# Gate weight sums by accumulating DMAs, and the fourth product added to the finished output

## The chip, the cores and the metric

The kernel runs on one core of a Trainium2 chip. The metric is the device time in microseconds (us) of one execution, the median of three runs. The core has TensorE (PE, with its weight loads PEld), VectorE (DVE), ScalarE (ACT), GpSimd (POOL) and SyncE (SP), and 16 DMA engines, which queues of SP, ACT and POOL feed. Each engine takes its instructions in order.

## The reference

One layer on x of 1024 tokens by 1024 channels in fp32. Two branches read the same normalised input, and per-channel gates merge them:

```python
xn = rmsnorm(x, norm1_g[layer])
u = xn @ w_in[layer].astype(f32)
...
o_sb = merge_heads(stick_breaking_attention(...))     # 8 heads of 64, in blocks of 128 queries
...
o_hg = rmsnorm(o_hg, ...)                             # HGRN2, 4 heads of 128
o_hg = merge_heads(o_hg) * jax.nn.silu(g_hg)
g_a = jax.nn.sigmoid(gate_sb + bg[:D_MODEL])
g_b = jax.nn.sigmoid(gate_hg + bg[D_MODEL:])
merged = g_a * (o_sb @ w_o_sb[layer]) + g_b * (o_hg @ w_o_hg[layer])
h = x + merged @ w_out[layer]
hn = rmsnorm(h, norm2_g[layer])
a = jnp.square(jax.nn.relu(hn @ w_ff1[layer]))
h = h + a @ w_ff2[layer]
return rmsnorm(h, final_g)
```

gate_sb, gate_hg (1024 columns each) and g_hg (512) are slices of u. They are matrix products of xn with columns of w_in, and these products are what the change is about.

## The kernel before, in words

**Products.** A matrix product in fp32 is made of three: both operands are split into a high part, which ACT copies (`hi_copy`), and a low part, which DVE subtracts (`lo_sub`), and PE adds up high x high, low x high and high x low in a PSUM bank of 128 x 512.

**Stages.** The program runs through: normalisation and transposes; attention, 8 heads of 8 query blocks, 64 items; HGRN2, head by head; the gates with the merge; the output product; the two MLP products; the last normalisation. Products that do not depend on the attention (the projections, the jobs `raw_job`, `q_job`, `f_job`) are laid in between the items by `st.advance`.

**The gates.** The columns of a gate product are taken in pairs of 128 columns: pair cb from 0 to 7 takes 128 columns of gate_sb and the same 128 of gate_hg; pairs 8 and 9 take four blocks of g_hg. The 2 x 2 block product (two halves of the 1024 rows of w_in, two column blocks, two halves of the tokens) is made by seven products in place of eight, which needs sums of the weights and of the inputs. The first half of the work (class `RawUnit`, `raw_job(cb)`), products 1, 2 and 4, runs early, beside attention and HGRN2; its results go to DRAM (`pd`, `gd`). The second half (class `GatePair`) runs in the gate stage with products 6, 5, 7 and 3: `x6`, `y5`, `x7`, `y3`. x6 and x7 add up in the bank gX, y5 and y3 in the bank gY, each of 12 matmuls. `RawUnit` subtracts weights on DVE into product 4's operand, in steps 4, 6 and 8 of the job (`split_t`); `GatePair.split` makes three subtractions of 512 columns on DVE for each pair. The inputs' sums (`sum_forms`) are made once. After x7 the sums with p1 and p14, which come back from DRAM as the tile pr, are made by DVE; after y3 the sum with u2 (gu).

**The order.** The pairs run 8, 9, 0, 4, 1, 5, 2, 6, 3, 7. For a pair of 0 to 7 an output product of the HGRN2 branch (`hg_product`, bank pyh, 12 matmuls) stands between x7 and y3. For pair 9 nothing stands there. Work of the next pair (the splits into tg, whig, wlog) is put behind `y_sum`, the first sum after x7. A scheduler sorts each engine's instructions by the dependencies and by those that `after` adds.

**POOL's queue.** In the attention POOL issues the copies that double a head's Q (L698: QH and QL, two halves of each head), clears small tiles, and issues the sums of the output weights (`out_weight_sums`, L1320: 32 DMAs of 256 KB into tw in DRAM, of which the last 16 add to what is there), one for every second item. A DMA that adds to a tile waits on POOL until the one before into this tile has landed.

Of the kernel before, what the change touches and what calls it, by code (L numbers as in the profile page):

```python
# [2 lines left out]

# [16 lines left out]
P = 128  # L20
# [19 lines left out]
def kernel(  # L40
# [462 lines left out]
    class Stream:  # L503
# [36 lines left out]
        def step(self):  # L540

            if self.gen is None:
                if self.pos >= len(self.jobs):
                    return False
                self.steps = 0
                self._start()
            self.steps += 1
            if self.owed_t and self.steps in (4, 6, 8):
                self.owed_t.split_t(hg_level[0] or turn_lo[0], self.steps // 2 - 1)
                if self.steps == 8:  # L550
                    self.owed_t = None
# [760 lines left out]
    def out_weight_sums():  # L1312
# [3 lines left out]
        for op, ways in ((ALU.bypass, plain), (ALU.add, summed)):  # L1316
            for i, src in ways:
                for r in range(4):
                    rs = slice(r * P, (r + 1) * P)
                    after(nc.gpsimd.dma_start(tw[i][rs], src[rs], accum_op=op), lastsel[0])  # L1320
                    yield

    def gate_bias(which, cb):
        return prm[:, BG + which * KT + cb : BG + which * KT + cb + 1]
# [8 lines left out]
    class RawUnit(Unit):  # L1333


        late = True
        turned = 0

        def __init__(self, cb):
            dmas = [  # L1340
                [(0, P, W_IN[:, gate_cols(w, cb)].rearrange("(k p) c -> p k c", p=P))]
                for w in range(2)
            ]
            super().__init__(f"wga{cb}", dmas)
            if cb < KT:
                self.roomy = (1,)

        def split(self):
            if self.hl is not None:
                return  # L1350
            self.load()
            ra, rb = self.raw
# [3 lines left out]
            hi_lo(h, l, ra)  # L1356
            self.hl = [(h, l)]

        def split_t(self, behind=None, upto=3):
            ra, rb = self.raw  # L1360
            while self.turned < upto:
                self.turned += 1
                if self.turned == 1:
                    after(sub(rb, ra, rb), behind)
                elif self.turned == 2:
                    after(sub(rb[:, 512:], rb[:, 512:], rb[:, 0:512]), behind)
                else:
                    t = slot(f"{self.name}t", F32R)
                    self.hl.append((t[:, 0:512], t[:, 512:]))
                    after(hi_lo(*self.hl[1], rb[:, 512:]), behind)  # L1370

    raw_units = [RawUnit(cb) for cb in range(NG)]

    def raw_job(cb):
# [13 lines left out]
        def body():  # L1388
            p1, p14, g1 = (half(f"{n}_{cb}") for n in ("p1", "p14", "g1"))
            ps, p4 = bank(f"pga{cb}"), bank(f"pgq{cb}")  # L1390
# [12 lines left out]
            hi_behind[0] = None  # L1403
            yield from steps_of(p4, 1, 0, 1, 4, True)
            add(p14, p1, p4)
            if cb == 3 or cb == KT - 1:
                whole_input(1, int(cb == KT - 1))
            nc.gpsimd.dma_start(pd[cb][:, 1, :], p14)
# [27 lines left out]
    def sum_forms():  # L1436
# [93 lines left out]
    class GatePair:  # L1530
# [3 lines left out]
        def load(self):  # L1534
# [3 lines left out]
            ]  # L1538
            for i, s_, which in ((0, 0, 0), (0, 1, 1), (1, 1, 1)):
                load(  # L1540
                    self.raw[i][:, s_ * 512 : (s_ + 1) * 512].rearrange("p (k c) -> p k c", k=4),
                    W_IN[i * 512 : (i + 1) * 512, gate_cols(which, cb)].rearrange(
                        "(k p) c -> p k c", p=P
                    ),
                )
            if cb >= KT:
# [17 lines left out]
        def split(self, behind=None):  # L1564
            cb = self.cb
            r0, r1 = self.raw
            s0, s1 = slice(0, 512), slice(512, 1024)
            first = behind if self is gates_in[3] else None
# [74 lines left out]
        def x7(self):  # L1643
            self.product(7, self.X, False)
            p1, p14 = self.p[:, 0:512], self.p[:, 512:1024]
            self.y_sum = add(p1, p1, self.Y)
            add(p1, p1, self.X)
            add(p14, p14, self.X)
            self.gate(p1, 1)
            self.gate(p14, 0)  # L1650

        def late_half(self):
# [3 lines left out]
            ps = self.hg_product(1)  # L1656
            p1, p14, y = self.p[:, 0:512], self.p[:, 512:1024], self.y[:, 512:1024]
            mul(y, y, p14)
            mul(p1, p1, ps)
# [749 lines left out]
    for h in range(NHG + 1):  # L2409
# [4 lines left out]
        while going:  # L2414
            going = False
            for g in (lev, tail):
# [112 lines left out]
```

## Time and profile before

| | |
|---|---|
| median of 3 runs | 1419.76 us (1419.64 to 1419.85) |
| the profiled execution's span | 1418.4 us, 18800 instructions |
| PE busy | 1408.7 us, 99% |
| DVE busy | 1086.9 us, 77% |
| ACT busy | 684.9 us, 48% |
| POOL busy | 147.3 us, 10% |
| granted TensorE clock, mean | 0.999 |
| HBM | 168.32 MB read, 66.06 MB written |

The median is 1.36 us above the span of the profiled execution; that much lies around the first and the last instruction. Times in the trace count from the start of the span. In a row of a timeline stand start, us, engine, line, operation, output <- input, and in brackets an idle time ahead of it with what ended it. In the chain of waits the pieces follow one another without gaps.

### The profile page before, as it was taken

To read this page: it belongs to the slowest core of one execution; us is meant where nothing else is said; L and a number is where in the kernel's file an instruction comes from. 1 tells how busy PE (TensorE), PEld (TensorE's weight loads), DVE (VectorE), ACT (ScalarE), POOL (GpSimd) and SP (SyncE) were. 2 spreads that over 40 slices of the span, in tenths; PEclk is the share of its full clock that TensorE was granted. 3 is DMA by queue.
4 is the path that set the end of the run, shared out by engine and by line. 5 is a ranking of instruction groups with operands and counts; after the bars stand their busy time and mean duration, and the time that the engine had idled before them with its cause. 6 is when DMAs were issued, how large, how long until landed. Compare 5 with 4: busy or idle time off the path is not lost.

```text
span 1418.4 us, 18800 instructions
## 1 busy us (share of the span) xinstructions
PE 1408.7 (99%) x6848; PEld 1183.6 (83%) x6848; DVE 1086.9 (77%) x1493; ACT 684.9 (48%) x1183; POOL 147.3 (10%) x341
## 2 busy tenths in 40 slices
PE   9999999999999999999999999999999999999998
PEld 7888888888888888888888888888888888888886
DVE  7679988988567888887788897676666657668765
ACT  6356676664243554433344764445444443534343
POOL 3012223210011031000000300000000000000042
PEclk9999999999999999999999999999999999999999
DMA  7124445535135685364585514444446974776725
GB/s 238 30 67 127 105 100 98 107 77 157 59 74 171 224 225 178 126 215 156 162 298 193 186 54 169 163 163 143 137 145 239 353 265 149 279 273 238 278 94 188
DMA packets 163173, 237.72 MB, mean 168 GB/s; under 512 B 26332, under 2 KB 93448, under 8 KB 163080
## 3 DMA queue, kind: packets, MB, share of 16 engines
q1 hardware_dynamic: 146056, 190.37, 40.0%
q0 software_dynamic: 11584, 34.61, 10.0%
q10 hardware_dynamic: 5440, 11.54, 2.3%
q8 instruction: 54, 0.88, 0.3%
q14 instruction: 39, 0.32, 0.1%
HBM read 168.32 MB, written 66.06 MB: 165 GB/s over the span
## 4 chain that ended last, share of the span: by engine, by line
PE 98%; DVE 1%; ACT 0%; POOL 0%; DMA 0%; issue 0%; POOLq 0%; SPq 0%; DVEq 0%
PE pm L128 21%; PE pX L128 9%; PE pW L128 6%; PE pY L128 6%; PE pjqk L128 6%; PE pga L128 4%; PE gX L128 4%; PE gY L128 4%; PE pjf L128 3%; PE pjq L128 3%; PE pys L128 3%; PE pji L128 3%; PE pyh L128 3%; PE pjv L128 3%; PE po L128 3%; PE z L128 2%
## 5 line engine op out<-in xcount | busy, mean ns | idle before, releaser
L156 ACT CAST whid<-w 128x1024 fp32r<-128x1024 f32 x30 | 31.6, 1053 | 154.5 <-PE pm L128 87.4
L831 DVE TENSOR_TENSOR_SCAN rm<-rm,bits 128x511 f32<-128x511 f32 (+7 forms) x72 | 87.3, 1219 | 16.4 <-ACT rm L809 16.4
L128 PE MATMUL pm<-wlod,sh 128*128 128x512 f32 x240 | 93.5, 390 | 0.0
L128 PE MATMUL pm<-whid,sl 128*128 128x512 f32 x240 | 93.4, 389 | 0.0
L128 PE MATMUL pm<-whid,sh 128*128 128x512 f32 x240 | 93.4, 389 | 0.0
L128 PE MATMUL pm<-tl,sh 128*128 128x512 f32 (+1 forms) x210 | 81.3, 387 | 0.0
L128 PE MATMUL pm<-th,sl 128*128 128x512 f32 (+1 forms) x210 | 81.3, 387 | 0.0
L128 PE MATMUL pm<-th,sh 128*128 128x512 f32 (+1 forms) x210 | 81.3, 387 | 0.0
L161 DVE TENSOR_TENSOR wlod<-w,whid 128x1024 fp32r<-128x1024 f32 x30 | 36.7, 1222 | 55.3 <-ACT whid L156 55.3
L161 DVE TENSOR_TENSOR sl<-sa,sh 128x1024 fp32r<-128x1024 f32 x56 | 68.2, 1218 | 0.0
L156 ACT CAST wTh<-pw 128x512 fp32r<-128x512 f32 (+2 forms) x96 | 43.8, 485 | 41.9 <-PE pw L131 41.0
L2148 POOL TENSOR_SCALAR fss<-fss 128x1 f32<-128x1 f32 x8 | 4.5, 561 | 562.0 <-ACT fsc L2143 561.5
L156 ACT CAST sh<-sa 128x1024 fp32r<-128x1024 f32 x56 | 57.2, 1046 | 7.2 <-DMA sa<-ad 7.2
L161 DVE TENSOR_TENSOR wTl<-pw,wTh 128x512 fp32r<-128x512 f32 (+2 forms) x96 | 49.9, 546 | 4.6 <-ACT wTh L156 4.4
L128 PEld LDWEIGHTS pm<-wlod,sh 128*128 128x128 f32 x240 | 45.1, 188 | 10.0 <-DVE wlod L161 0.4
L128 PEld LDWEIGHTS pm<-whid,sh 128*128 128x128 f32 x240 | 45.0, 188 | 9.5
L128 PEld LDWEIGHTS pm<-whid,sl 128*128 128x128 f32 x240 | 45.0, 188 | 9.1
L169 DVE TENSOR_TENSOR bt<-bt,rm 128x511 f32<-128x511 f32 (+7 forms) x72 | 48.9, 684 | 3.5
L809 ACT ACTIVATE rm<-z 128x511 f32<-128x511 f32 (+4 forms) x96 | 48.0, 500 | 5.5 <-PE z L128 2.8
L128 PE MATMUL pX<-sqh,t1l 128*128 128x512 f32 x128 | 49.9, 390 | 0.0
L128 PE MATMUL pX<-sql,t1h 128*128 128x512 f32 x128 | 49.9, 390 | 0.0
L128 PE MATMUL pX<-sqh,t1h 128*128 128x512 f32 x128 | 49.8, 389 | 0.0
(932 smaller groups left out, 4434.8 us busy)
## 6 DMA issues: line engine op xcount, KB each, us to landing
w<-in_w_ff_dram SPq DMA_DIRECT2D x72, 512.0 KB, 4.8
sa<-ad SPq DMA_DIRECT2D x52, 512.0 KB, 6.4
ad<-a SPq DMA_DIRECT2D x32, 256.0 KB, 4.3
ad<-s SPq DMA_DIRECT2D x16, 512.0 KB, 3.3
tw<-in_w_out_dram POOLq DMA_DIRECT2D x24, 256.0 KB, 4.6
pr<-pd SPq DMA_DIRECT2D x10, 512.0 KB, 6.0
x<-in_x_dram SPq DMA_DIRECT2D x8, 512.0 KB, 7.8
xnl<-xnh POOLq DMA_DIRECT2D x8, 512.0 KB, 6.5
```

The source lines that it names most:

```text
L128: return pe(nc.tensor.matmul(*a, **k))
L156: hi_last[0] = after(in_turn("act", nc.scalar.copy(dst, src)), hi_behind[0])
L161: nc.vector.tensor_tensor(out=dst, in0=src, in1=hi.bitcast(F32), op=ALU.subtract),
L169: return nc.vector.tensor_tensor(out=out, in0=a, in1=b, op=ALU.mult)
L809: nc.scalar.activation(rm[:, s0 + c0 - 1 : s0 + m - 1], z[:, c0:m], AF.Sigmoid, scale=-0.125)
L831: sc = nc.vector.tensor_tensor_scan(out=rr, data0=rr, data1=bits[:, 1024 - nk + a : 1024 - nk + b][:, ::-1], initial=rm[:, b : b + 1] if i ...
L2148: nc.gpsimd.tensor_scalar(out=ssq, in0=ssq, scalar1=1.0 / D, scalar2=EPS, op0=ALU.mult, op1=ALU.add)
```

## The change

It does four things.

1. The sums of weights for the gates are made in DRAM by DMAs of POOL, `gate_weight_sums`: 43 DMAs of 512 KB into tg1 to tg4 (tg1 and tg3 lie in one tensor tg13), one after each item of the attention. First come four for the g_hg columns of tg4 (one writes, three add), then 32 for the blocks of 128 x 1024, then seven for the g_hg columns of tg1, tg3 and tg2. The 32 DMAs for the output weights follow behind, also one by one, the last of them in the loop over the HGRN2 heads.
2. The signs are turned so that all sums of weights are additions: `sum_forms` and the sums after the products get other signs. DVE's subtractions of weights go; `RawUnit` loads 512 and 256 KB in place of 1 MB, `GatePair` 512, 256 and 256 KB, and `split_t` runs once, in step 6.
3. The fourth product goes to DRAM by itself (p4, copied by ACT) instead of added to the first (p14, added by DVE). In `x7` it is added to the finished p1.
4. `raw_job(KT)` and `q_job(0)` change places among the jobs of heads 2 and 4.

**POOL around the first copies of head 1.** tg4 is the tile of the new sums in DRAM, tw that of the output weights' sums, QH1 and QL1 are head 1's copies, two halves each. Rows of small memsets are left out. Before:

```order
L698 DMA QH1_874<-QH1_874 64x512 [waits DVE_49,Activation_49]
L698 DMA QL1_875<-QL1_875 64x512 [waits DVE_49,PE_49]
L1320 DMA tw_131<-in_w_out_dram 128x512
L698 DMA QH1_874<-QH1_874 64x512 [waits Activation_49]
L1320 DMA tw_131<-in_w_out_dram 128x512 [waits DMASW0_49]
L698 DMA QL1_875<-QL1_875 64x512 [waits DMASW1_49,DVE_49]
```

Now:

```order
L1337 DMA tg4_144<-in_w_in_dram 512x2x128
L698 DMA QH1_876<-QH1_876 64x512 [waits DVE_49,Activation_49]
L698 DMA QL1_877<-QL1_877 64x512 [waits DVE_49,PE_49]
L1337 DMA tg4_144<-in_w_in_dram 512x2x128 [waits DMASW4_49]
L1337 DMA tg4_144<-in_w_in_dram 512x2x128 [waits DMASW7_49,DMASW0_49]
L698 DMA QH1_876<-QH1_876 64x512 [waits DMASW1_49,Activation_49]
L1337 DMA tg4_144<-in_w_in_dram 512x2x128 [waits DMASW2_49,DMASW0_49]
L698 DMA QL1_877<-QL1_877 64x512 [waits DMASW3_49,DVE_49]
```

Before, two writes to tw that wait for nothing but a free semaphore stood between the copies; now three DMAs that add to tg4 stand there, each waiting for a DMA ahead of it, and the last copy of QL1 stands behind the third of them.

**DVE after x7 of pair 9.** pr9 holds p1 and p4 (p14), gX9 and gY9 are the banks, gu9 is u2, tgl0 a weight split of the next pair, ahgl1 a part of HGRN2's output. Before:

```order
L1289 TENSOR_TENSOR pr9_5777<-pr9_5777,gY9_5916 128x512 [waits DVE_49,PE_49]
L161 TENSOR_TENSOR ahgl1_5913<-on1_4493,ahgh1_5912 128x1024 [waits Activation_49]
L161 TENSOR_TENSOR tgl0_5937<-wg0r0_5781,tgh0_5936 128x1024 [waits Activation_49]
L1289 TENSOR_TENSOR pr9_5777<-pr9_5777,gX9_5891 128x512 [waits DVE_49,PE_49]
L1289 TENSOR_TENSOR pr9_5777<-pr9_5777,gX9_5891 128x512
L1289 TENSOR_TENSOR gu9_5904<-gu9_5904,gY9_5916 128x512 [waits PE_49]
```

Now:

```order
L162 TENSOR_TENSOR ahgl1_5933<-on1_4536,ahgh1_5932 128x1024 [waits Activation_49]
L162 TENSOR_TENSOR tgl0_5954<-wg0r0_5801,tgh0_5953 128x1024 [waits DMAHW5_49,Activation_49]
L1289 TENSOR_TENSOR pr9_5797<-pr9_5797,gX9_5911 128x512 [waits PE_49]
L1289 TENSOR_TENSOR pr9_5797<-pr9_5797 128x512 [waits DVE_49]
L1292 TENSOR_TENSOR pr9_5797<-gY9_5936,pr9_5797 128x512 [waits DVE_49]
L1292 TENSOR_TENSOR gu9_5924<-gY9_5936,gu9_5924 128x512 [waits PE_49]
```

Before, gY9 was read ahead of the two splits and gX9 twice after them; now gX9 is read once, the second sum is of pr9 alone, and gY9 is read third. y3 adds into gY9 and waits for that.

**DVE after x7 of pair 0.** wg4 holds the weights of pair 4, the next one, wlog4 and tgl4 are its splits. Before:

```order
L1289 TENSOR_TENSOR pr0_5944<-pr0_5944,gY0_6019 128x512 [waits DVE_49,PE_49]
L161 TENSOR_TENSOR ahgl3_6016<-on3_5494,ahgh3_6015 128x1024 [waits Activation_49]
L1289 TENSOR_TENSOR pr0_5944<-pr0_5944,gX0_5994 128x512 [waits DVE_49,PE_49]
L1289 TENSOR_TENSOR pr0_5944<-pr0_5944,gX0_5994 128x512
L1292 TENSOR_TENSOR wg4r0_5948<-wg4r0_5948 128x512 [waits DMAHW7_49,DMAHW6_49]
```

Now:

```order
L162 TENSOR_TENSOR ahgl3_6033<-on3_5520,ahgh3_6032 128x1024 [waits Activation_49]
L1289 TENSOR_TENSOR pr0_5961<-pr0_5961,gX0_6011 128x512 [waits PE_49]
L162 TENSOR_TENSOR wlog4_6067<-wg4r1_5966,whig4_6066 128x1024 [waits DMAHW7_49,DMAHW0_49]
L1289 TENSOR_TENSOR pr0_5961<-pr0_5961 128x512 [waits DVE_49]
L162 TENSOR_TENSOR tgl4_6071<-wg4r0_5965,tgh4_6070 128x1024 [waits DMAHW6_49,Activation_49]
L1292 TENSOR_TENSOR pr0_5961<-gY0_6036,pr0_5961 128x512 [waits DVE_49]
```

Before, gY0 was read ahead of gX0. Now the two splits of pair 4 stand between the three sums, and the read of gY0 is the last.

The diff, cut to its core:

```diff
-            if self.owed_t and self.steps in (4, 6, 8):
-                self.owed_t.split_t(hg_level[0] or turn_lo[0], self.steps // 2 - 1)
-                if self.steps == 8:
-                    self.owed_t = None
+            if self.owed_t and self.steps == 6:
+                self.owed_t.split_t(hg_level[0] or turn_lo[0])
+                self.owed_t = None
...
+    TGW = NG * P
+    tg13 = dram("tg13", [1024, TGW])
+    tg = {1: tg13[0:512], 3: tg13[512:1024]}
+    tg.update({i: dram(f"tg{i}", [512, TGW]) for i in (2, 4)})
+
+    def gate_weight_sums():
+        def gh(i, which):
+            rows = W_IN[i * 512 : (i + 1) * 512, C_GH : C_GH + HGW]
+            return rows.rearrange("k (c w p) -> w k c p", w=2, p=P)[which]
...
+        def add_up(dst, src, op=ALU.add):
+            after(nc.gpsimd.dma_start(dst, src, accum_op=op), lastsel[0])
+
+        for t, terms in (
+            (4, ((0, 0), (0, 1), (1, 0), (1, 1))),
+            (1, ((0, 0), (0, 1))),
+            (3, ((0, 1), (1, 1))),
+            (2, ((0, 0), (0, 1), (1, 1))),
+        ):
+            if t == 1:
+                yield from block_sums(range(4))
+            for j, (i, which) in enumerate(terms):
+                add_up(gh_of(tg[t]), gh(i, which), ALU.add if j else ALU.bypass)
+                yield
+
+    def block_sums(rows):
...
+        for t, op, src in (
+            (1, ALU.bypass, (0, 0)),
+            (3, ALU.bypass, (0, 1)),
+            (1, ALU.add, (0, 1)),
+            (3, ALU.add, (1, 1)),
+            (2, ALU.bypass, 1),
+            (2, ALU.add, (1, 1)),
+            (4, ALU.bypass, 2),
+            (4, ALU.add, (1, 0)),
+        ):
+            for r in rows:
+                s_ = part(src, r) if type(src) is int else block(*src, r)
+                after(nc.gpsimd.dma_start(part(t, r), s_, accum_op=op), lastsel[0])
+                yield
...
-            add(p14, p1, p4)
+            nc.scalar.copy(p4, pq)
...
-            ins = add(s1[kp], raw[1, 0, kp], raw[1, 1, kp])
+            ins = sub(s1[kp], raw[1, 0, kp], raw[1, 1, kp])
...
-            sub(s4, raw[0, 1, kp], s2[kp])
+            add(s4, raw[0, 1, kp], s2[kp])
...
         if h == 2:
+            q_job(0)
+        if h == 4:
             raw_job(KT)
-        if h == 4:
-            q_job(0)
...
-            after(sub(r0[:, s0], r0[:, s1], r0[:, s0]), first)
-            sub(r1[:, s0], r1[:, s1], r0[:, s0])
...
-            sub(r0[:, s1], r1[:, s1], r0[:, s1])
...
         def x7(self):
             self.product(7, self.X, False)
-            p1, p14 = self.p[:, 0:512], self.p[:, 512:1024]
-            self.y_sum = add(p1, p1, self.Y)
-            add(p1, p1, self.X)
-            add(p14, p14, self.X)
+            p1, p4 = self.p[:, 0:512], self.p[:, 512:1024]
+            self.y_sum = add(p1, p1, self.X)
+            add(p4, p4, p1)
+            sub(p1, self.Y, p1)
             self.gate(p1, 1)
-            self.gate(p14, 0)
+            self.gate(p4, 0)
...
             self.product(3, self.Y, False)
-            add(self.u2, self.u2, self.Y)
+            sub(self.u2, self.Y, self.u2)
...
-    wsums = out_weight_sums()
+    wsums = chain(gate_weight_sums(), out_weight_sums())
...
-        if i % 2 == 1:
-            next(wsums, None)
+        next(wsums, None)
...
                 if next(g, StopIteration) is not StopIteration:
                     going = True
+                    next(wsums, None)
```

More of the change, by code (lines that the diff above doesn't have):

```diff
@@ L2 @@
 from contextlib import ExitStack
+from itertools import chain
 import concourse.bass as bass
@@ L1321, in out_weight_sums, with gh_of, block, part @@
                     yield
+    TGW = NG * P
[6 more added lines that the diff above has]
+            return rows.rearrange("k (c w p) -> w k c p", w=2, p=P)[which]
+        def gh_of(t):
+            return t[:, KT * P :].rearrange("k (c p) -> k c p", p=P)
+        def add_up(dst, src, op=ALU.add):
[12 more added lines that the diff above has]
+    def block_sums(rows):
+        def block(i, which, r):
+            c0 = (C_GA, C_GB)[which]
+            return W_IN[i * 512 + r * P : i * 512 + (r + 1) * P, c0 : c0 + D]
+        def part(t, r):
+            return tg[t][r * P : (r + 1) * P, 0:D]
+        for t, op, src in (
[12 more added lines that the diff above has]
+                yield
+    def gate_sum(t, cb):
+        return t[:, cb * P : (cb + 1) * P].rearrange("(k p) c -> p k c", p=P)
     def gate_bias(which, cb):
@@ L1336, with load @@
         late = True
-        turned = 0
+        turned = False
         def __init__(self, cb):
[L1340 to L1346, printed above, removed]
+            src = W_IN[:, gate_cols(0, cb)].rearrange("(k p) c -> p k c", p=P)
+            super().__init__(f"wga{cb}", [[(0, P, src)]])
+            self.cb = cb
+        def load(self):
+            if self.raw is not None:
+                return
+            super().load()
+            if self.cb < KT:
+                t = slot(f"{self.name}r1")
+            else:
+                t = wpool.tile([P, 1024], F32, tag="raw", name=f"{self.name}r1")
+            load(t[:, 0:512].rearrange("p (k c) -> p k c", k=4), gate_sum(tg[4], self.cb))
+            self.raw.append(t)
         def split(self):
@@ L1351, in split @@
             self.load()
-            ra, rb = self.raw
             h, l = (
@@ L1355, in split, with split_t @@
             )
-            hi_lo(h, l, ra)
+            hi_lo(h, l, self.raw[0])
             self.hl = [(h, l)]
[L1359 to L1370, printed above, removed]
+        def split_t(self, behind=None):
+            if not self.turned:
+                self.turned = True
+                t = slot(f"{self.name}t", F32R)
+                self.hl.append((t[:, 0:512], t[:, 512:]))
+                after(hi_lo(*self.hl[1], self.raw[1][:, 0:512]), behind)
     raw_units = [RawUnit(cb) for cb in range(NG)]
@@ L1388, in body @@
         def body():
-            p1, p14, g1 = (half(f"{n}_{cb}") for n in ("p1", "p14", "g1"))
-            ps, p4 = bank(f"pga{cb}"), bank(f"pgq{cb}")
+            p1, p4, g1 = (half(f"{n}_{cb}") for n in ("p1", "p4", "g1"))
+            ps, pq = bank(f"pga{cb}"), bank(f"pgq{cb}")
             if 6 <= cb < KT:
@@ L1403, in body @@
             hi_behind[0] = None
-            yield from steps_of(p4, 1, 0, 1, 4, True)
-            add(p14, p1, p4)
+            yield from steps_of(pq, 1, 0, 1, 4, True)
+            nc.scalar.copy(p4, pq)
             if cb == 3 or cb == KT - 1:
                 whole_input(1, int(cb == KT - 1))
-            nc.gpsimd.dma_start(pd[cb][:, 1, :], p14)
+            nc.gpsimd.dma_start(pd[cb][:, 1, :], p4)
             yield from steps_of(ps, 0, 4, 0, 4, False)
@@ L1538, in load @@
             ]
[L1539 to L1545, printed above, removed]
+            r0, r1 = (r.rearrange("p (k c) -> p k c", k=8) for r in self.raw)
+            load(r0, gate_sum(tg13, cb))
+            load(r1[:, 0:4], gate_sum(tg[2], cb))
+            load(r1[:, 4:8], W_IN[512:, gate_cols(1, cb)].rearrange("(k p) c -> p k c", p=P))
             if cb >= KT:
@@ L1567, in split @@
             s0, s1 = slice(0, 512), slice(512, 1024)
-            first = behind if self is gates_in[3] else None
-            after(sub(r0[:, s0], r0[:, s1], r0[:, s0]), first)
-            sub(r1[:, s0], r1[:, s1], r0[:, s0])
             h, l = (
@@ L1656, in late_half @@
             ps = self.hg_product(1)
-            p1, p14, y = self.p[:, 0:512], self.p[:, 512:1024], self.y[:, 512:1024]
-            mul(y, y, p14)
+            p1, p4, y = self.p[:, 0:512], self.p[:, 512:1024], self.y[:, 512:1024]
+            mul(y, y, p4)
             mul(p1, p1, ps)
```

## The prediction

> **What bounds the kernel now.** I read the page first, then the waits of PE, then busy time in stretches of 50 us, and then the two places that the change touches.
>
> ```profile
> span 1418.4 us, 18800 instructions
> PE 1408.7 (99%) x6848; PEld 1183.6 (83%) x6848; DVE 1086.9 (77%) x1493; ACT 684.9 (48%) x1183; POOL 147.3 (10%) x341
> PE 98%; DVE 1%; ACT 0%; POOL 0%; DMA 0%; issue 0%; POOLq 0%; SPq 0%; DVEq 0%
> ```
>
> PE is busy for 1408.7 of 1418.4 us and carries 98% of the chain. DVE has 23% of the span free. The waits of PE (engine, line, what it waited for: us in total, times, longest) and the stretches (us of busy time in 50; column 2 is PE, then PEld, DVE, ACT, POOL, the granted clock, the DMA engines' share, GB/s) say how little is left:
>
> ```profile
> PE warm L128 <- POOL ident masks.py:199: 2.2, 1, 2.2
> PE po L128 <- DVE wTl L161: 0.3, 1, 0.3
> PE pjqk L128 <- DVE xnl L351: 0.3, 1, 0.3
> PE xnt L131 <- DVE xnl L351: 0.2, 1, 0.2
> ```
>
> ```profile
> 50.00:100.00 50.00, 49.69 (x248) 41.75 (x247) 30.92 (x46) 24.57 (x54) 6.23 (x22) 1.00 0.16 43
> 100.00:150.00 50.00, 50.00 (x289) 43.25 (x287) 46.65 (x66) 35.62 (x81) 13.37 (x48) 1.00 0.54 130
> 200.00:250.00 50.00, 50.00 (x293) 43.57 (x292) 45.53 (x61) 34.26 (x80) 16.13 (x46) 1.00 0.59 106
> 250.00:300.00 50.00, 50.00 (x286) 43.13 (x285) 44.06 (x63) 35.69 (x83) 10.40 (x39) 1.00 0.41 74
> 550.00:600.00 50.00, 50.00 (x227) 41.37 (x226) 41.58 (x57) 20.91 (x30) 4.01 (x5) 1.00 0.52 167
> 600.00:650.00 50.00, 50.00 (x222) 41.42 (x221) 42.80 (x63) 16.89 (x23) 2.96 (x6) 1.00 0.59 191
> ```
>
> In the attention (100 to 300) and in the gates (550 to 750) PE has no idle time at all, at a granted clock of 1.00. The change leaves the matmuls as they are. So DVE work that it takes away was hidden behind PE everywhere but in the waits on DVE above, 0.8 us together, of which only the 0.3 for wTl comes after the point where the change begins. **The gain is at most 0.3 us; all that can move the time is new waiting of PE.** I look for that.
>
> **DVE and ACT.** Out go some 60 DVE operations: three subtractions of 512 columns for each of ten gate pairs, two for each of ten first halves, ten additions of the fourth product. The ten additions become ten ACT copies of a bank. All of it lies under a PE that does not wait, and ACT is busy for 20.91 of 50 us in the gates; I cost it at nothing. SP's queue gets shorter loads in the gates (1 MB in place of 1.5 for a pair); nothing on PE waited for them, so no gain.
>
> **The order at the end of x7: a new wait.** Formerly the bank gY was read before x7 ended, and after x7 only gX was read, twice. Now DVE first adds gX into p1, then adds p1 to p4, and only the third operation reads gY. The next product, y3, accumulates into gY, and so its first matmul cannot start before that third operation. Around the second pair, cb 9, the chain of waits of PE, DVE's timeline, and PE's timeline at the turn from x7 to y3 (start, us) read:
>
> ```profile
> 579.53 2.72 PE gY L128 x12
> 582.25 2.72 PE gX L128 x12
> 584.97 2.72 PE gY L128 x12
> ```
>
> ```profile
> 583.11 0.68 DVE L1289 TENSOR_TENSOR pr<-pr,gY 128x512 f32<-128x512 f32 x1
> 583.71 1.22 DVE L161 TENSOR_TENSOR ahgl<-on,ahgh 128x1024 fp32r<-128x1024 f32 x1
> 584.86 1.22 DVE L161 TENSOR_TENSOR tgl<-wg0r,tgh 128x1024 fp32r<-128x1024 f32 x1
> 585.99 1.28 DVE L1289 TENSOR_TENSOR pr<-pr,gX 128x512 f32<-128x512 f32 x2
> ...
> 588.33 1.29 DVE L169 TENSOR_TENSOR pr<-pr,gs 128x512 f32<-128x512 f32 x2
> ```
>
> ```profile
> 584.35 0.39 PE L128 MATMUL gX<-gsl,tgh 128*128 128x512 f32 x1
> 584.58 0.39 PE L128 MATMUL gX<-gsh,tgl 128*128 128x512 f32 x1
> 584.80 0.39 PE L128 MATMUL gY<-gsh,whig 128*128 128x512 f32 x1
> ```
>
> x7's last matmul starts at 584.58 and ends 0.39 later, at 584.97. y3 follows 0.22 after it with nothing between: this pair has no output product to cover the gap. In the new order DVE comes to x7's sums behind ahgl and tgl; with the gY addition ahead of them gone, ahgl starts at 583.11, tgl at 584.26, the first sum at 585.39. Each of the three reads what the one before wrote, so I take 0.69 each (the length of one; two independent ones take 1.28): the third ends at 585.39 + 2.07 = 587.46. y3's first matmul then starts one weight load later, 0.23, at 587.69 instead of 584.80: **2.9 us**. If DVE had been free at 584.97 it would be 584.97 + 2.07 + 0.23 - 584.80 = 2.5; that is the lower bound.
>
> The next pair is cb 0. Now an output product, pyh, stands between x7 and y3:
>
> ```profile
> 593.13 2.72 PE gX L128 x12
> 595.85 2.72 PE pyh L128 x12
> 598.57 2.72 PE gY L128 x12
> ```
>
> ```profile
> 594.27 1.22 DVE L161 TENSOR_TENSOR ahgl<-on,ahgh 128x1024 fp32r<-128x1024 f32 x1
> 595.89 1.28 DVE L1289 TENSOR_TENSOR pr<-pr,gX 128x512 f32<-128x512 f32 x2 [0.40 <-PE gX L128]
> ...
> 644.85 1.29 DVE L1289 TENSOR_TENSOR pr<-pr,gX 128x512 f32<-128x512 f32 x2 [0.68 <-PE gX L128]
> ```
>
> DVE gets the first sum at 595.89. But the order puts a weight split (wlog of pair 4) between the first and the second sum and another (tgl) between the second and the third. A neighbour of 512 columns costs 0.60 from start to start, one of 1024 columns 1.15 (583.71 to 584.86). So the gY read ends at 595.89 + 0.60 + 1.15 + 0.60 + 1.15 + 0.69 = 600.08, and y3, whose piece began at 598.57 less the 0.17 by which pieces in the chain lie behind the starts (584.97 against 584.80), thus at 598.40, starts at 600.08 + 0.23 = 600.31: **1.9 us**. Without the two splits it would be 595.89 + 2.07 + 0.23 = 598.19, within the cover. So for the other seven pairs with pyh behind x7 and the three sums next to each other (as at 644.85) the cover holds by 0.2 us; I take 0.2 us for all seven together, and 0 to 1 as bounds. cb 8, whose x7 is followed by other products, costs nothing. **Gates: 2.9 + 1.9 + 0.2 = 5.0 us, bounds 4.1 and 6.**
>
> **POOL's queue in the attention.** The sums are DMAs in POOL's queue, one per item of attention (43 of them), where before one of 256 KB went out every second item. The first four add up the gh columns of tg4: 512 x 2 runs of 128 floats, 1024 pieces of 512 B. Three of them add, and each waits on POOL until the one before has landed. Behind them stand the copies QH and QL of head 1. From POOL's timeline, PE's, and the landings of those copies (the first of the two lines for 80 to 84 us, the second for 88 to 93):
>
> ```profile
> 82.94 0.57 POOL L1320 DMA_DIRECT2D tw<-in_w_out_dram  x1
> ...
> 89.09 0.53 POOL L698 DMA_DIRECT2D QH<-QH  x1 [4.91 <-ACT QH L156]
> ...
> 91.00 0.53 POOL L698 DMA_DIRECT2D QL<-QL  x1 [0.71 <-DVE QL L161]
> ```
>
> ```profile
> 99.55 0.48 PE L128 MATMUL z<-KS,QH 128*128 128x512 f32 x1
> 99.87 0.39 PE L128 MATMUL z<-KS,QL 128*128 128x512 f32 x1
> ```
>
> ```profile
> DMA to landing us min/median/max: 2.1/2.2/2.2
> ```
>
> ```profile
> DMA to landing us min/median/max: 2.2/2.5/2.9
> ```
>
> QL was issued at 91.00 and landed about 93.3 to 93.9; head 1's first scores need it at 99.55 (the QL matmul at 99.87). That leaves 6 us. Now the second piece of the sum goes out where tw did, at 82.94, the third when it has landed, the fourth when the third has landed, and QL behind the fourth. With L for one landing, the fourth goes out at 82.94 + 2L. Its packets and QL's are in one queue; I take QL to land behind it (the 2.9 above, with a tw 1.26 us ahead, against 2.2 alone is a weak sign of that): 82.94 + 3L + 0.6 for the issue. PE waits **3L - 16.0 us** if that is positive.
>
> What is L? No add of small pieces is in the trace. The queues' packets (count, MB, share of 16 engines' span) and two groups of DMAs (KB each, median us to landing):
>
> ```profile
> q1 hardware_dynamic: 146056, 190.37, 40.0%
> q0 software_dynamic: 11584, 34.61, 10.0%
> ```
>
> ```profile
> tw<-tw POOLq DMA_DIRECT2D x8, 256.0 KB, 6.2
> QL<-QL POOLq DMA_DIRECT2D x16, 128.0 KB, 2.2
> ```
>
> A packet of q1 took 0.400 x 16 x 1418.4 / 146056 = 62 ns at 1303 B; one of q0 took 196 ns at 2988 B. 1024 pieces are 64 for each of 16 engines. The fixed part lies between the copies' whole landing, 2.2, and that of the add tw<-tw without its packets (128 rows of 2 KB, 8 for each engine: 6.2 - 8 x 0.196 = 4.6). Low end: q0 by bytes, 34 ns a piece: L = 2.2 + 2.2 = 4.4, no wait at all. High end: 196 ns a piece whatever its size: L = 4.6 + 12.5 = 17.1, a wait of 35. I take the 62 ns of the smaller packets and the middle of the fixed parts: L = 3.4 + 4.0 = 7.4, **a wait of 6.2 us**. If QL isn't held back by the fourth piece, it lands 0.6 + 2.2 behind its issue, at 82.94 + 14.8 + 2.8 = 100.5, and the wait is under 1 us.
>
> [...]
>
> **The block sums.** 32 DMAs of 512 KB follow, 4-KB rows, 8 packets for each engine. By q0's bytes a packet takes 196 x 4096 / 2988 = 269 ns, so one DMA takes 2.1 us of each engine. 64 items in the 250 us or so of attention are 3.9 us each, a share of 0.55; the tw sums had 8 x 0.134 us in two items, 0.14. On the 0.41 to 0.59 of the stretches that makes 0.82 to 1.0. The engines have just room; the copies of heads 2 to 7 will land later, by one such DMA in front, some 2 to 4 us. Head 1's had 6 us to spare in the tighter place; I take 0 here, with a bound of 5.
>
> **Sum.** 1418.4 + 5.0 + 6.2 = 1429.6 for the profiled execution. The median of the runs is 1.36 us above its span, so **1431.0** for the median.
>
> **Rivals.**
>
> *Only the gates.* The small adds land within 5.3 us each, or QL overtakes. For it: the copies' 2.2 us. Then 1419.76 + 5.0 = 1424.8, up to 1427 with a wait of 1 or 2 for QL. [...]
>
> *The DMA engines are the bound.* Adds take near 196 ns a piece (L of 11 to 17: a wait of 17 to 35), or the block sums pile up until copies come late for some heads. For it: a share near 1.0. Against it: q1's 62 ns, and slack after head 1. 1419.76 + 5 + 17 = 1442, up to 1460.
>
> *Not slower.* Matmuls run faster when DVE and the DMAs use the memories less. Place: the gate stage; price: to bring 5.0 us down below 2.8, the stage's some 170 us of matmuls would have to run 1.3% quicker, and the adds would have to be free. Against it: all pieces of 12 matmuls above take 2.72 us, beside a busy DVE and beside an idle one. It would give 1419.5 to 1422.5.
>
> **Chances and range.** 0.2% of the time, 2.8 us, is about what a measurement can tell from no change. Forecast (1427.5 to 1436) 0.45; only the gates (1423 to 1427.5) 0.27; DMA engines (1436 to 1460) 0.21; not slower 0.07. The first three are all slower by over 0.2%: 0.93. Of the rest, 0.05 within 0.2%, 0.02 faster. The range leaves out the lowest tenth and the highest tenth: 1423.5 to 1444.
>
> **What would show it.** In the waits of PE: gY behind DVE's sum, one wait of 2.9 and one of 1.9 us, the gY read as DVE's third operation after x7; z of head 1 waiting on the DMA of QL, 6 us near 100 us, with POOL's three gh adds each going out about 7.4 us after the one before. Whether QL lands behind the fourth gh DMA or ahead of it. In the stretches from 100 to 250 a DMA share of 0.8 to 1.0 and no further wait of z. DVE's busy time lower by some 45 us with nothing gained. It is wrong if PE waits elsewhere (a pair other than 9 and 0, a later head), or if the time is within 2.8 us of before.

## The result, and the profile after

The changed kernel takes **1453.78 us** (median of 4 runs, 1452.55 to 1455.97) against 1419.78 us before: ratio 1.0241, 95% interval 1.0226 to 1.0255. It is 34.0 us slower, three times the forecast's 11. The profiled execution's span is 34.5 us longer. Of all runs in this text one is left out, of the kernel with wide rows below, which took 2025.49 us at a mean granted clock of 0.655. The page of the profiled execution:

```profile
span 1452.9 us, 18795 instructions
PE 1419.0 (98%) x6848; PEld 1189.3 (82%) x6848; DVE 1052.0 (72%) x1433; ACT 690.2 (48%) x1193; POOL 190.8 (13%) x384
PE 89%; DMA 4%; issue 2%; DVE 2%; POOL 1%; ACT 1%; SPq 0%; POOLq 0%; ACTq 0%; DVEq 0%
```

DVE is busy for 35 us less, as the change means it to be. PE, with the same 6848 matmuls, is busy for **10.3 us more**, and its share of the chain has fallen from 98% to 89%. Two things have to be found: idle time of PE, and matmuls that take longer. The waits of PE (us in total, times, longest) are these:

```profile
PE z L129 <- DMA QL<-QL: 7.4, 1, 7.4
PE gY L129 <- DVE pr L1292: 4.7, 2, 3.2
PE sd L129 <- ACT sd_h L157: 4.1, 2, 3.5
PE po L129 <- POOL wTh L867: 3.1, 2, 1.9
PE pw L132 <- POOL bt L813: 2.3, 1, 2.3
...
PE po L129 <- DVE wTl L162: 1.3, 1, 1.3
PE sd L129 <- DVE sd_l L162: 0.5, 2, 0.3
```

They sum up to 23.4 us; before, only one wait of this kind stood there, 0.3 us at wTl. z and gY were forecast. sd, the two at POOL's memsets and one at wTl were not.

**The longer matmuls.** The table cuts the trace of PE into windows of 3.41 us, the step in which its granted clock changes in this trace: from 7.21 us on it stands at one value for 98.99, 6.83, 146.77 and 3.41 us, which are 29, 2, 43 and 1 of them. Columns: window, its length, busy time (matmuls), granted clock, DMA share, GB/s.

```profile
106.19:109.60 3.41, 1.02 (x3) 0.50 1.16 348
109.60:113.02 3.42, 3.42 (x10) 0.50 1.02 416
...
256.38:259.79 3.41, 1.56 (x13) 1.00 0.41 113
259.79:263.21 3.42, 3.42 (x11) 0.50 1.08 143
...
351.95:355.36 3.41, 0.64 (x2) 1.00 0.98 96
355.36:358.78 3.42, 2.50 (x5) 0.50 1.06 337
...
611.36:614.78 3.42, 1.68 (x8) 1.00 0.00 0
614.78:618.19 3.41, 1.94 (x8) 1.00 0.73 207
```

After a window in which PE was busy for 1.56 of 3.41 us (256.38), the next one runs at a clock of 0.50: 11 matmuls in it where a full one has 20 or so. After one of 1.68 (611.36) it does not. The half clock lasted until a window had 3.30 us or more of work, and went on after one of 2.50: 106.19 to 113.02, 259.79 to 263.21, 270.03 to 273.45, 355.36 to 362.19. PE is busy for 17.1 us in these (20.5 less 3.4 idle) and does half of it: 8.5 of the 10.3 us. So a wait cost its own length, and the four that left PE idle for 1.85 us or more of one such window cost 1.7 to 3 us more each.

**Where the waits come from.** POOL's timeline at the first and at the last sums of g_hg columns (start, us, engine, line; in brackets the idle time ahead and what ended it):

```profile
82.73 2.44 POOL L1337 DMA_DIRECT2D tg<-in_w_in_dram  x1
...
91.12 2.30 POOL L1337 DMA_DIRECT2D tg<-in_w_in_dram  x1 [5.55 <-DMA tg<-in_w_in_dram]
...
100.12 2.31 POOL L1337 DMA_DIRECT2D tg<-in_w_in_dram  x1 [5.74 <-DMA tg<-in_w_in_dram]
101.41 1.59 POOL L698 DMA_DIRECT2D QL<-QL  x1
...
245.36 2.33 POOL L1337 DMA_DIRECT2D tg<-in_w_in_dram  x1 [6.34 <-DMA tg<-in_w_in_dram]
...
256.29 2.31 POOL L1337 DMA_DIRECT2D tg<-in_w_in_dram  x1 [5.22 <-DMA tg<-in_w_in_dram]
257.59 1.23 POOL L867 MEMSET wTh<- 128x128 f32 x1
...
267.13 2.29 POOL L1337 DMA_DIRECT2D tg<-in_w_in_dram  x1 [7.85 <-DMA tg<-in_w_in_dram]
268.40 1.58 POOL L698 DMA_DIRECT2D QH<-QH  x1
```

At the start, each sum goes out 8.4 to 9.0 us after the one before, and QL, last in the queue, lets z go at 108.58. At the end the same happens again with the last seven: POOL stands still four times (6.00, 6.34, 5.22 and 7.85 us), and behind the last two stands PE needs memsets that come after the waiting DMAs. The gates, as forecast (DVE's timeline after x7 of pair 9):

```profile
612.93 1.22 DVE L162 TENSOR_TENSOR tgl<-wg0r,tgh 128x1024 fp32r<-128x1024 f32 x1
614.06 0.68 DVE L1289 TENSOR_TENSOR pr<-pr,gX 128x512 f32<-128x512 f32 x1
614.78 0.69 DVE L1289 TENSOR_TENSOR pr<-pr 128x512 f32<-128x512 f32 x1
615.51 0.69 DVE L1292 TENSOR_TENSOR pr<-gY,pr 128x512 f32<-128x512 f32 x1
```

The wait of sd comes from a load (chain of waits, HGRN2 stage):

```profile
340.15 10.01 DMA wir<-in_w_in_dram
...
350.23 1.05 ACT wih L157
...
353.82 0.63 ACT sd_h L157
```

ACT and DVE stand in front of wir's splits and do not come to sd's. wir took 10.9 us to land, 3.9 before. From 317 to 354 us POOL issued 18 of the DMAs for the output weights, nearly in one burst, and from 320 to 348 us the DMA share was 1.03 to 1.15.

By cause, in the profiled execution, half clock included: start of the sums 0.9 (po: 1.23, less the 0.32 that PE waited at wTl in the same place before) + 7.45 (z) + 2.2 (half clock) = 10.6; end of the sums 1.85 + 2.33 + 3.4 = 7.5; wir 4.6 + 2.9 = 7.6; gates 4.75 + 0.7 (the piece behind each wait takes 3.05 in place of 2.72) = 5.4; wTl at 178 us 1.25, where DVE had waited for a late copy od (below). That is 32.4 of 34.5.

### The profile page after: what moved, and what is told of

It reads as the page before. It is cut to its first block, busy times and chain, and to the rows that moved or that the text cites. A ratio compares the mean times of both kernels' runs of the same rounds, so it can differ in the third digit from the quotient of the medians.

```text
span 1452.9 us, 18795 instructions
## 1 busy us (share of the span) xinstructions
PE 1419.0 (98%) x6848; PEld 1189.3 (82%) x6848; DVE 1052.0 (72%) x1433; ACT 690.2 (48%) x1193; POOL 190.8 (13%) x384
## 4 chain that ended last, share of the span: by engine, by line
PE 89%; DMA 4%; issue 2%; DVE 2%; POOL 1%; ACT 1%; SPq 0%; POOLq 0%; ACTq 0%; DVEq 0%
PE pm L129 21%; PE pX L129 9%; PE pW L129 6%; PE pY L129 6%; PE pjqk L129 4%; PE pga L129 4%; PE gY L129 3%; PE gX L129 3%; PE pji L129 3%; PE pys L129 3%; PE pyh L129 3%; PE pjq L129 3%; PE pjv L129 3%; PE pjf L129 3%; PE pwX L129 2%
## 5 line engine op out<-in xcount | busy, mean ns | idle before, releaser
L157 ACT CAST wTh<-pw 128x128 fp32r<-128x128 f32 (+3 forms) x96 | 44.0, 486 | 46.8 <-PE pw L132 43.1
```

The lines of the kernel that those rows point to most:

```text
L157: hi_last[0] = after(in_turn("act", nc.scalar.copy(dst, src)), hi_behind[0])
```

## The experiments

Each ran on the chip beside runs of the kernel before (1419.97 to 1420.01 us there). All ratios are to it.

### The read order in x7 undone

```diff
-            self.y_sum = add(p1, p1, self.X)
-            add(p4, p4, p1)
-            sub(p1, self.Y, p1)
+            add(p4, p4, p1)
+            self.y_sum = sub(p1, self.Y, p1)
+            sub(p1, p1, self.X)
+            add(p4, p4, self.X)
```

> Only x7's sums are put in another order, so that gY is read before x7 ends: p4 += p1, p1 = gY - p1 (both can run before x7 is done), then p1 -= gX, p4 += gX; four operations where the change has three. Theory (the third-in-line read of gY makes y3 wait): the two waits of gY on DVE (3.2 and 1.5 us in the changed kernel) vanish, and the 0.3 us by which the first piece after each is longer: about 5.4 us less than the changed kernel, near 1448.4. Rival (DVE is late there for another reason, the wait only changes its name): gY or the next gX still waits 3 us or more in all, 1452 to 1455.

Measured 1447.38 us (1.0193, 1.0177 to 1.0209), 6.4 less than the changed kernel, where about 5.4 was expected. No wait of gY is left in PE's list, and y3 of pair 9 follows x7 in the chain at 608.42 with no gap, 2.72 long:

```profile
605.70 2.72 PE gX L129 x12
608.42 2.72 PE gY L129 x12
```

The order of three DVE operations made the waits. One more DVE operation for each pair brought no wait. The 6.4 us are not the gates alone: the four runs spread from 1444.8 to 1450.1, and in the profiled one the waits of sd are 3.2 us in place of 4.6.

### The g_hg sums kept apart

```diff
+        blocks = block_sums(range(4))
...
             for j, (i, which) in enumerate(terms):
                 add_up(gh_of(tg[t]), gh(i, which), ALU.add if j else ALU.bypass)
                 yield
+                for _ in range(3):
+                    if next(blocks, StopIteration) is not StopIteration:
+                        yield
```

> Only the order of the 43 DMAs for gate weights is changed: one of the eleven for g_hg columns, then three block sums, and so on, so that none waits on POOL for one just issued. Same bytes, same pieces. Theory (POOL stands still at a DMA that waits for the one before, and copies and memsets stand behind it): the wait of z for QL (7.4 us), those for wTh and bt memsets (1.2, 1.9 and 2.3) and the half clock behind them (some 5.6 us lost) vanish: about 18 us less than the changed kernel, 1435.7. Rival (the DMA engines are full, whatever the order): copies are late for other heads, the waits of z, po and pw sum up to 8 us or more, 1445 or above.

Measured 1435.77 us (1.0106, 1.0089 to 1.0123): 18.0 less, as worked out. PE's list has no z, no wTh and no bt any more; beside 1.0 at wTl it reads:

```profile
PE gY L129 <- DVE pr L1292: 4.7, 2, 3.2
PE sd L129 <- ACT sd_h L157: 3.6, 2, 2.8
```

The same bytes in the same pieces, with other DMAs between a sum and the next that needs it, cost 18 us less. So these waits came from the order in POOL's queue, not from the traffic. The DMA engines are no emptier here (share 1.05 from 150 to 200 us, against 0.91 in the changed kernel).

### The output weights' sums moved

```diff
-                    after(nc.gpsimd.dma_start(tw[i][rs], src[rs], accum_op=op), lastsel[0])
+                    after(nc.gpsimd.dma_start(tw[i][rs], src[rs], accum_op=op), last_power[0])
...
-                    next(wsums, None)
+                    if last_power[0] is not seen:
+                        seen = last_power[0]
+                        for _ in range(4):
+                            next(osums, None)
```

> Only the 32 DMAs for the output weights are moved: none in the attention, four behind each of the eight small norm operations of POOL in the HGRN2 stage, 430 to 580 us. Theory (their burst, 325 to 352 us, fills the DMA engines just when the wir weights are loaded, 10.9 us in place of 3.9): wir lands in 4 to 5 us, the waits of sd (4.6 us) and the half clock behind them (2.9) vanish: 7.5 us less, 1446.3. Rival (wir is late since its buffer or SP's queue comes late, by the changed order of jobs): the wait of sd stays, 1452 to 1455.

Measured 1460.77 us (1.0288, 1.0272 to 1.0303): the wait of sd is gone, as the theory has it, but the kernel is slower by 7 than the changed one, where 7.5 less was expected. PE's list shows why:

```profile
PE sl L129 <- ACT ksl L1067: 6.6, 1, 6.6
PE gY L129 <- DVE pr L1292: 4.7, 2, 3.2
...
PE gX L129 <- DVE gu L1289: 4.0, 1, 4.0
```

Both new waits follow loads or copies that now land late (chain of waits):

```profile
527.59 17.00 DMA xnl<-xnh
...
576.87 17.28 DMA wg9r<-in_w_in_dram
```

The burst only changed its place and found other victims. So I put the sums where the engines were empty: the trace of the run with the sums kept apart shows shares of 0.46 and 0.26 from 250 to 300 us.

```diff
         next(wsums, None)
+        if i >= 43:
+            next(wsums, None)
```

> The changed kernel, and only the output weights' DMAs come two per item from item 43 on, none in the HGRN2 stage. Theory (their burst at the end of the attention delays the load of wir): the wait of sd near 350 us and its half clock vanish, 7.5 us less, 1446. Rival (any place costs as much): other copies or loads come late, 1452 or more.

Measured 1448.10 us (1.0196, 1.0181 to 1.0212), 5.7 less than the changed kernel, where 7.5 was expected. wir lands in 3.7 us, and no wait of sd is left; in turn the wait at the bt memset, at the end of the g_hg sums, is 4.3 us (2.3 in the changed kernel):

```profile
DMA to landing us min/median/max: 3.7/3.7/3.7
```

```profile
PE pw L132 <- POOL bt L813: 4.3, 1, 4.3
```

### The jobs changed back

```diff
         if h == 2:
-            q_job(0)
+            raw_job(KT)
         if h == 4:
-            raw_job(KT)
+            q_job(0)
```

> Only raw_job(KT) and q_job(0) change back to heads 2 and 4. Theory (the swap costs nothing): the time stays within 1.5 us of the changed kernel, 1452 to 1455, and the wait of sd near 350 us stays. Rival (the swap brought the loads of the HGRN2 stage out of step): the wait of sd goes, 1446.

Measured 1450.60 us (1.0225, 1.0203 to 1.0247). The load of tg4's g_hg columns then stands in the program ahead of three of the four sums, so the first half of pair 8 reads an unfinished sum: the swap is needed for the change to compute the right thing. The swap makes little of the loss: z waits 6.9 us, gY 4.7, sd 3.0, and po for a memset 3.6. The expectation, within 1.5 us of the changed kernel, was missed by 1.7, but the two intervals overlap, and the runs spread from 1449.4 to 1457.0. In the profiled execution, one of the shortest, the wait at bt is missing, and those at wTl, z and sd are shorter.

### All of the repairs together

The read order, the sums kept apart and the output weights two per item, in one kernel.

> The changed kernel with gY read before x7 ends, the g_hg DMAs kept apart by three block sums, and the 32 DMAs for the output weights issued two per item from item 43 on, so that they are over before the HGRN2 stage loads its weights. Theory (all of the loss is waits of PE that these places make, and the half clock behind them): PE waits 1 to 2 us in all past the start, no half clock past 20 us, 1420 to 1422.5. And since DVE has some 35 us less to do than in the kernel before, a time within 0.2% of before says that this relief buys nothing. Rival (the extra 22 MB of DMA traffic cost by themselves): 1425 or more, with waits for DMAs at other places.

Measured 1421.33 us (10 runs, 1420.94 to 1421.56; 1.0010, 1.0000 to 1.0019), 32.5 less than the changed kernel. Its page, and the one wait of PE past the start with what stands behind it on DVE:

```profile
PE 1408.0 (99%) x6848; PEld 1183.3 (83%) x6848; DVE 1054.9 (74%) x1443; ACT 689.4 (49%) x1193; POOL 186.8 (13%) x384
```

```profile
PE po L129 <- DVE wTl L162: 1.4, 1, 1.4
```

```profile
161.05 1.02 DVE L162 TENSOR_TENSOR wTl<-pw,wTh 128x512 fp32r<-128x512 f32 x2 [2.03 <-DMA od<-osb]
```

PE is busy for as long as before. No half clock is left between the start and the end. The 1.4 us that remain are about the one wait of 1.4: DVE waited for a copy od, which took 7.6 us to land (2.9 to 3.6 in the kernel before) in a stretch with a DMA share of 1.05. So the traffic itself seems to cost something, through that copy; no run tries it by itself. DVE has 32 us less to do than before, and the kernel is not faster.

### The first four sums alone

The kernel before, with the four DMAs into tg4 added at the first four items.

```diff
-        if i % 2 == 1:
+        if i < 4:
+            next(gsums, None)
+        elif i % 2 == 1:
             next(wsums, None)
```

> The kernel before, and only the first four g_hg DMAs of the change added, at the first four items; their sums are not used. The output weights' sums start after them. Theory (POOL's queue order alone makes the wait): z waits for QL 6.5 to 8 us, po for a memset about 1, and the half clock behind costs 2 to 3.5: 1430 to 1432. Rival (the copies were late since the block sums behind them fill the DMA engines): QL lands in 2 to 4 us, no wait over 3 us, 1420 to 1424.

Measured 1432.51 us (1.0088, 1.0071 to 1.0105), 12.5 more than before. z waits 8.7 us; PE is busy for 2.9 us more, with the clock at 0.50 from 105.32 to 115.56.

```profile
82.68 2.44 POOL L1331 DMA_DIRECT2D tg<-in_w_in_dram  x1
...
90.94 2.30 POOL L1331 DMA_DIRECT2D tg<-in_w_in_dram  x1 [5.42 <-DMA tg<-in_w_in_dram]
...
99.02 2.31 POOL L1331 DMA_DIRECT2D tg<-in_w_in_dram  x1 [4.82 <-DMA tg<-in_w_in_dram]
100.31 1.59 POOL L698 DMA_DIRECT2D QL<-QL  x1
```

There are no block sums in this kernel: the chain of four makes the wait by itself. QL went out at 100.31 and let z go at 109.34, 9.0 us later: it was held back behind the fourth sum, as the forecast took it, since alone it lands in 2.2. The trace's packet records agree: the 1024 packets of the fourth sum start between 103.1 and 108.3.

### The same chain with wide rows

As the run before this, with 128 rows of 4 KB in place of 1024 pieces of 512 B.

```diff
-            src = rows.rearrange("k (c w p) -> w k c p", w=2, p=P)[which]
-            dst = tg4[:, KT * P :].rearrange("k (c p) -> k c p", p=P)
+            src = W_IN[i * 512 : i * 512 + P, c0 : c0 + D]
+            dst = tg4[0:P, 0:D]
```

> The kernel before with four chained DMAs at the first four items, as in the run with the g_hg DMAs alone and of the same 512 KB each, but in 128 rows of 4 KB in place of 1024 pieces of 512 B; their sums are not used. Theory (the small pieces make the landing long: 70 ns for each of 64 pieces on an engine, against 8 rows of some 0.3 us): a landing takes 5 to 6.5 us in place of 8.3, z waits 0 to 3.5 us by 3 L - 16, and the time is 1420 to 1425. Rival (the wait for a landing costs what it costs, whatever the pieces): z waits 7 us or more, 1430 or above.

Measured 1423.0 us (median of nine runs, 1422.0 to 1424.44; ratio 1.0024, 1.0014 to 1.0033). A sum goes out 6.2 us after the one before, z waits 2.3 us:

```profile
82.77 0.97 POOL L1331 DMA_DIRECT2D tg<-in_w_in_dram  x1
88.92 0.81 POOL L1331 DMA_DIRECT2D tg<-in_w_in_dram  x1 [4.50 <-DMA tg<-in_w_in_dram]
95.16 0.85 POOL L1331 DMA_DIRECT2D tg<-in_w_in_dram  x1 [4.74 <-DMA tg<-in_w_in_dram]
```

By 3 L - 16.0 with L = 6.2 the wait would be 2.6; with the 8.1 to 8.3 us of the run before it 8.3 to 8.9, where 8.7 was measured. The formula comes near for both sizes of piece, in the run before partly by luck: there QL let z go about a us later than the formula has it, and PE's idle time began at 100.68, about a us later than the formula's 99.55. The pieces of 512 B cost 2 us per landing. Most of that lies ahead of the first packet, not in the time of the pieces as was expected: by the packet records of the second and third sum, the first packet starts 3.0 to 3.2 us after the issue (1.5 to 1.7 with the wide rows), and the packets take 4.2 to 4.4 us (3.5 to 3.7). Issuing is dearer too: POOL starts its next instruction 1.3 us after a DMA of 1024 pieces, and 0.6 after one of 128 rows.

### Only the order of the three sums

The kernel before, with gY as the third of x7's sums.

```diff
-            self.y_sum = add(p1, p1, self.Y)
-            add(p1, p1, self.X)
+            self.y_sum = add(p1, p1, self.X)
             add(p14, p14, self.X)
+            add(p1, p1, self.Y)
```

> The kernel before, and only the order of x7's three sums is the change's: first gX into p1, then gX into p14, then gY into p1. Theory: y3 of pair 9 waits for DVE, 2.8 to 3.2 us; at pair 0 the three sums stand next to each other here and the output product covers them, so nothing there; 0.3 us for the piece behind. If the wait falls into one of the 3.41 us windows by which the clock is granted for more than half of it, 1.7 us of half clock come on top. 1423.0 without, 1425 with it. Rival (the waits in the gates come from the later arrival of the sums' tiles, not from the order): no wait, 1420.

Measured 1425.62 us (1.0040, 1.0025 to 1.0055), 5.6 more. y3 of pair 9 waits 2.95 us, pair 0 has no wait, pair 4 one of 0.31, and the clock is 0.50 from 588.41 to 591.83:

```profile
585.95 1.28 DVE L1289 TENSOR_TENSOR pr<-pr,gX 128x512 f32<-128x512 f32 x2
587.15 0.68 DVE L1289 TENSOR_TENSOR pr<-pr,gY 128x512 f32<-128x512 f32 x1
```

```profile
587.88 0.50 PE L128 MATMUL gY<-gsh,whig 128*128 128x512 f32 x1 [2.95 <-DVE pr L1289]
```

One line moved down by two costs 5.6 us of 1420, nearly half of it behind the wait, most of that by the clock. That pair 0 is free of a wait here shows that there the two splits between the sums made it, not the third place alone.

### DVE's relief alone

The kernel before, with four of five subtractions of weights cut from 512 or 1024 columns to 64. The gates' weights are then not what the reference has.

```diff
-            after(sub(r0[:, s0], r0[:, s1], r0[:, s0]), first)
+            after(sub(r0[:, n0], r0[:, n1], r0[:, n0]), first)
...
-            sub(r0[:, s1], r1[:, s1], r0[:, s1])
+            sub(r0[:, n1], r1[:, n1], r0[:, n1])
```

> The kernel before with four of the five subtractions of weights for each pair of gate columns cut to 64 columns, so the gates' weights are not what the reference has; nothing else is changed. DVE has some 25 us less to do. Theory (DVE's work was hidden behind PE): 1419.7 to 1420.3, no change. Rival (the relief brings its own gain, which the waits of the change hid): 1 us or more faster, 1419 or below.

Measured 1419.67 us (11 runs; 0.9997, 0.9988 to 1.0006). DVE is busy for 1065.3 us in place of 1086.9, and the time is the same. What the change was to relieve was not what the kernel waits for.

## Why the prediction was wrong, point by point

The direction was right; the size was not: 1431.0 was forecast, with a range up to 1444, and 1453.78 measured.

- **"The gain is at most 0.3 us."** Right. 22 us less of DVE work gave 0.3 us with an interval across zero, and the repaired kernel has no gain. DVE's busy time fell by 35 us, not by some 45, which no term of the sum rests on.
- **Gates, 5.0 us (2.9 + 1.9 + 0.2).** Right: 3.2 + 1.5, and nothing at the other pairs; with 0.7 for the slow pieces behind them 5.4, and 6.4, with shorter waits of sd in it, by the run that undoes it.
- **First sums, L = 7.4 and a wait of 6.2 us.** The mechanism was right, with QL held back behind the fourth sum; L was mis-sized, 8.4 to 9.0 (8.1 to 8.3 with the first four sums alone). The 64 pieces were nearly right, 4.2 to 4.4 us in the packet records where 4.0 was taken; the fixed part is the larger miss, some 3.9 where 3.4 was taken. The wait is 7.45, near the forecast partly by luck: with these L the formula gives 9.2 to 11, but PE's idle time began at 101.13 and not at 99.55, in good part because a memset had held up PE. The term had neither that memset's wait, 0.9, nor the half clock behind, 2.2.
- **"The block sums ... I take 0 here, with a bound of 5."** This is the step that failed. It priced only the traffic behind the first four sums and followed POOL's queue no further: the last seven g_hg DMAs, at the end of the same queue, hold up POOL as the first four do, and behind them stood memsets that PE needed. Measured: 7.5 us where 0 was put. By the prediction's own last sentence it is wrong if PE waits elsewhere, and it does.
- **The output weights' sums behind them.** This is the other failure: they had no price in the sum at all, and no reason is given for it. Pushed back by 43 items they came nearly in one burst beside the loads of the HGRN2 stage: 7.6 us in the profiled execution, 5.7 net by the run that moves them.
- **The granted clock.** The sum had PE wait at full clock. 8.5 us of matmuls at half clock, counted in the terms above, are the largest part of the 10.3 us in which PE was busy longer.
- **Rivals.** The time is that of the DMA-bound rival (1436 to 1460, chance 0.21), but for the most part not by its mechanism: a piece of the first four sums took 70 ns on average, not 196, and from 100 to 250 us the DMA share was 0.74, 0.91 and 0.79 in stretches of 50 us. With the same traffic in another order the kernel is 18 us faster, with all three orders mended 32.5. Full engines did play a part at wir, where the share was 1.03 to 1.15, but through a burst that only the order made, and not by the block sums that the rival names. With the orders mended, the one wait of 1.4 us is what may be left of that rival. The rival that only the gates cost, at 0.27, fell with QL's 7.4; the one of not slower with the pieces of 2.72 us, which a lighter DVE left at 2.72.

What stays open are some 2 us of the 34.5.

## What to carry to other kernels

Where one engine is busy all the time, as PE is here, work taken off another bought nothing (22 us less on DVE, ratio 0.9997), and what matters is which new thing that engine may come to wait for: ask it of every operation that changes its place in an in-order queue. A DMA that must wait for what another DMA wrote held up all that stood behind it on POOL for a whole landing, 8.1 to 9.0 us here, so put as many other DMAs between the two as a landing takes, at the end of a series as much as at its start. And the waits of the changed kernel that left PE idle for 1.85 us or more of one clock window of 3.41 cost 1.7 to 3 us more than their length, so a wait that can't be avoided is best kept short.

## What the runs showed of the hardware

**In these traces the granted clock changed in steps of 3.41 us, and the least idle time in one of them that was followed by half the clock was 1.85 us.** In each of the nine traces in which the clock fell between the start and the end, its changes lie on a grid of 3.41 us. In the changed kernel it fell after windows with 3.41 us idle (from 102.78 on), 1.85 (256.38), 2.21 (266.62) and 2.76 (351.95), and not after those with 1.74 (611.36), 1.65 (99.37) and 1.54 (628.43), of which the first was idle for a little over half. In the nine together, 24 windows at full clock in which PE was idle for 1.85 us or more were followed by one at half clock; 43 with more than 0.3 us of idle time, up to 1.87, were not (the next below are 1.74 and 1.65). From half clock it came back after windows with at most 0.61 us idle, and stayed after windows with 0.60 or more. The grid does not lie at the same place in every span: the first record at full clock starts at 6.74 us in the kernel before and at 7.21 in the changed one. The same wait of 3.21 us at gY fell across two windows in the changed kernel (1.74 and 1.47 us idle) and cost no clock; in the run with the sums kept apart 2.58 of it fell into one window, and the clock was halved for 6.8 us. Kernels with several waits spread by 3 us and more from run to run (the changed one 1452.55 to 1455.97, that with the jobs changed back 1449.4 to 1457.0), where the one before spreads by 0.2; whether the place of the grid makes this was not tried, and is not shown.

**After a sum of 1024 pieces POOL started its next instruction 1.3 us later, and the rows behind it were longer.** With the first four sums alone one went out at 82.68 and the memset behind it started at 84.00; with sums of 128 wide rows the two stand at 82.77 and 83.36, 0.6 apart. The rows of the memsets behind the sums of 1024 pieces are longer too: those of 128 x 1 take 1.1 to 1.2 us there (1.23 at 84.29), and 0.12 at 82.65, just ahead of the sum. They still start 0.04 to 0.15 us apart, so what comes later is their end. POOL's spans are rough, so I take no more from them.
